# Down product of a split-precision feed-forward layer: right operands split where they are made, sums evicted by three engines

## The chip, the cores and the metric

The kernel runs on one core of a Trainium2 chip. The metric is device time in microseconds (us); the kernel before took 2532.09 us (median of three runs, 2531.11 to 2537.94).

## The reference

One encoder layer over two groups of sequences (256 and 1024 tokens, each with 16 learned meta tokens ahead), width D = 1024, everything in float32. The change lies in the two feed-forward halves:

```python
h = h + 0.5 * _swiglu(_rmsnorm(h, norm_ffn1), ffn1_w_gate, ffn1_w_up, ffn1_w_down)
...                                   # u = rmsnorm(h) @ w_in; attention and pooling; h += mix @ w_out
h = h + 0.5 * _swiglu(_rmsnorm(h, norm_ffn2), ffn2_w_gate, ffn2_w_up, ffn2_w_down)
h = _rmsnorm(h, norm_final)

def _swiglu(x, w_gate, w_up, w_down):         # w_gate, w_up: 1024 x 2816, w_down: 2816 x 1024
    return (jax.nn.silu(x @ w_gate) * (x @ w_up)) @ w_down
```

## The kernel before

**Precision.** A float32 product is three matmuls (`mm3`, lines 161 to 163): each operand is a sum of a high part (a cast to the format fp32r) and a low part (the operand minus its high part), and high times high, low times high and high times low are accumulated. The high part of an operand is a cast on ScalarE (`hi_act`, line 146), the low part a subtraction on VectorE (`lo_dve`, line 152) or GpSimd (`lo_pool`, line 155). The pair of instructions is called a split below.

**Seven products.** Each of gate, up and down is done as a fast two by two block product with 7 products in place of 8 (`seven`, line 441): the operands' quarters are combined by sums and differences (weights in `s_parts`, right operands named b11, t1, t2, b22, t3, b21, t4 in that order), and the results are combined in place. `PRODUCTS` gives each product one of the accumulators A, B, C: A takes b11, t2, t3 and t4 in turn, C takes t1 and b22, so that a sum must be read out of PSUM before the next product may add to the same bank. Right operands come in two halves, s = 0 and 1, of two token groups each; one tile is 128 by 324 (first layer half, FFN1) or 128 by 320 (FFN2). Reading a sum out of its PSUM bank is called an eviction.

**Gate and up** (`gate_up`, line 457). 11 passes j, each of a gate and an up product (14 weight parts, 84 matmuls for each half and product). The first three j run for one half at a time (half 0 first, and half 1 after the other eight), beside which the right operands of the other half are formed; the other eight run for both. `after` in `product` drains sums by ScalarE (line 503) or adds them on VectorE (line 509); `up` multiplies by the gate and forms the down product's right operands b11 to t4, each of which goes to device memory as one float32 tile (`out`, line 469; the names hid_d4b and hid_d4t in rows are such tiles of j = 4: b for b11, b22 and b21, t for t1 to t4).

**Down** (`down_tasks`, line 532; the loop is `run_`). The 11 j make six slices: slice 0 holds one j (j = 3), slices 1 to 5 two each. In a slice, 4 blocks mp of two output chunks of 128 follow one another, each with 7 products and two halves: 84 matmuls, 42 in slice 0. A block splits its seven weight parts (ring buffers `wh`, `wl`, and the sums `ws`), and every product's sums go into h in SBUF by one VectorE instruction, h = 0.5 * bank + h (line 616, `after`); `ADDS` says which part of h: b11 and b21 share one, t1 and t3, t2 and b22. Each right operand is loaded as float32 (`load`, line 539, tile `raw`, four buffers, SP's queue) and split (`split`) into pool `x` (10 slots, for five operands of the second j in a slice) or `y` (32 slots in FFN1, 26 in FFN2). `work` does one load and split behind each product in the first three blocks of a slice, and four behind each in the last, and the rest after it. Since slots of `x` and most of `y` come free only as the slice's last block uses them, most splits of a slice lie at its border with the slice ahead.

**Order.** The kernel is written as one stream of instructions for a scheduler that gives each engine its own order from priorities and the times that buffers come free; what follows from that is shown in rows of the order below. All loads and writes named here are issued by SyncE (SP), in one queue, in order: an issue that waits holds those behind it.

## Time and profile before

| what | value |
|---|---|
| median of three runs | 2532.09 us |
| profiled execution, its own time | 2531.91 us |
| its span | 2529.8 us |
| granted clock of TensorE, mean | 0.963 |
| TensorE (PE) busy, matmuls | 2325.6 us (92%) |
| VectorE (DVE) busy | 1753.6 us (69%) |
| ScalarE (ACT) busy | 985.5 us (39%) |
| GpSimd (POOL) busy | 274.8 us (11%) |
| data moved | 308.48 MB, mean 122 GB/s |

The span is the time from the first to the last instruction of the profiled execution; 2.1 us of its own time lie around it. FFN1's gate and up passes run from the start to about 627 us, its down product from there to about 940; the mixer with attention follows, then FFN2's gate and up passes, and its down product from 2177 us to the end. A stretch is read as: its length, then each engine's busy time with the count of its instructions, the clock granted to TensorE as a share of the full one, the share of the DMA engines' time and the rate. An engine's busy time over a stretch's length says how much room it has there.

### The profile page before, as it was taken

The numbers are of one execution on the slowest core, as the hardware profiler recorded it, in microseconds if no ns is written. First come the engines' busy times: TensorE is split into PE (matmuls) and PEld (weight loads), VectorE is DVE, ScalarE is ACT, GpSimd is POOL, SyncE is SP. The second block draws the span as 40 slices with busy tenths as digits, with TensorE's granted clock in tenths as the row PEclk, the third lists the DMA queues.
The fourth block names the chain that finished last, engine by engine and source line by source line (L and its number), as shares of the span: only waits on it lengthen the run. The fifth ranks groups of instructions, "written<-read, shape, count | busy, mean of one in ns | idle before, by whom it ended". The sixth has DMA issues, their size and how long they took to land.

```text
span 2529.8 us, 42335 instructions
## 1 busy us (share of the span) xinstructions
PE 2325.6 (92%) x15434; PEld 2264.9 (90%) x15434; DVE 1753.6 (69%) x3850; ACT 985.5 (39%) x2247; POOL 274.8 (11%) x342
## 2 busy tenths in 40 slices
PE   5899999999799998999888898899999999888897
PEld 5899999999699998899878898889999999788897
DVE  6965546558999996443477747685465557898997
ACT  6533333334433343111366733353333334433433
POOL 0000000000000013111366743000000000000000
PEclk7999999999899998999999999999999999999998
DMA  8323222354544423563654154432223227434432
GB/s 226 117 88 111 79 81 95 108 175 143 145 128 112 116 92 95 154 215 101 176 138 127 48 160 153 132 109 87 84 98 100 71 87 237 135 117 126 127 102 84
DMA packets 351236, 308.48 MB, mean 122 GB/s; under 512 B 29004, under 2 KB 337316, under 8 KB 350516
## 3 DMA queue, kind: packets, MB, share of 16 engines
q1 hardware_dynamic: 351028, 305.79, 39.9%
q8 instruction: 121, 1.98, 0.3%
q14 instruction: 87, 0.71, 0.1%
HBM read 212.55 MB, written 97.37 MB: 123 GB/s over the span
## 4 chain that ended last, share of the span: by engine, by line
PE 69%; DVE 14%; DMA 9%; ACT 3%; issue 3%; POOL 2%; SPq 1%; ACTq 0%; POOLq 0%; DVEq 0%
PE bank L162 22%; PE bank L161 22%; PE bank L163 21%; DVE h L616 3%; DVE wl L152 3%; DMA v<-v_d 2%; ACT wh L146 1%; DVE yl L152 1%; PE pair L957 1%; DMA wraw<-in_ffn_w_up 1%; PE bank L1005 1%; PE pair L958 1%; PE bank L242 1%; DVE xl L152 1%; DMA wraw<-in_ffn_w_gate 1%
## 5 line engine op out<-in xcount | busy, mean ns | idle before, releaser
L152 DVE TENSOR_TENSOR wl<-wraw,wh 128x512 fp32r<-128x512 f32 (+2 forms) x374 | 220.8, 600 | 271.7 <-ACT wh L146 216.6
L146 ACT CAST wh<-ws 128x512 fp32r<-128x512 f32 (+2 forms) x414 | 211.7, 513 | 448.9 <-PE bank L163 256.5
L162 PE MATMUL bank<-yh,wl 128*128 128x324 f32 (+1 forms) x1128 | 358.1, 318 | 16.5 <-DVE wl L152 16.4
L161 PE MATMUL bank<-yh,wh 128*128 128x324 f32 (+1 forms) x1128 | 341.6, 321 | 25.8 <-DVE h L616 12.0
L163 PE MATMUL bank<-yl,wh 128*128 128x324 f32 (+1 forms) x1128 | 353.4, 315 | 0.0
L616 DVE SCALAR_TENSOR_TENSOR h<-bank,h 128x324 f32<-128x324 f32 (+1 forms) x672 | 321.4, 489 | 30.8 <-PE bank L163 24.2
L152 DVE TENSOR_TENSOR wl<-ws,wh 128x512 fp32r<-128x512 f32 (+2 forms) x414 | 229.5, 557 | 79.0 <-ACT wh L146 77.2
L161 PEld LDWEIGHTS bank<-yh,wh 128*128 128x128 f32 x1128 | 211.5, 193 | 40.5 <-ACT wh L146 15.0
L162 PEld LDWEIGHTS bank<-yh,wl 128*128 128x128 f32 x1128 | 217.0, 192 | 23.8 <-DVE wl L152 21.8
L503 ACT COPY hid<-bank 128x324 f32<-128x324 f32 (+1 forms) x264 | 112.8, 428 | 291.2 <-PE bank L163 260.9
L163 PEld LDWEIGHTS bank<-yl,wh 128*128 128x128 f32 x1128 | 216.4, 192 | 0.6 <-POOL yl L155 0.5
L509 DVE TENSOR_TENSOR hid<-bank,hid 128x324 f32<-128x324 f32 (+1 forms) x264 | 129.4, 490 | 83.7 <-PE bank L163 77.2
L146 ACT CAST wh<-wraw 128x512 fp32r<-128x512 f32 (+2 forms) x310 | 153.6, 513 | 47.5 <-PE bank L163 40.1
L162 PE MATMUL bank<-xh,wl 128*128 128x324 f32 (+1 forms) x472 | 152.1, 323 | 17.6 <-DVE wl L152 17.6
L161 PE MATMUL bank<-xh,wh 128*128 128x324 f32 (+1 forms) x472 | 148.2, 324 | 5.5 <-DVE h L616 3.8
L163 PE MATMUL bank<-xl,wh 128*128 128x324 f32 (+1 forms) x472 | 150.2, 319 | 0.0
L161 PE MATMUL bank<-t1h,wh 128*128 128x324 f32 (+1 forms) x352 | 112.3, 320 | 19.9 <-ACT wh L146 19.9
L146 ACT CAST yh<-raw 128x324 fp32r<-128x324 f32 (+1 forms) x188 | 84.8, 460 | 104.2 <-DMA raw<-hid_d4b 11.6
L223 POOL TENSOR_TENSOR ry<-rv,neg_half 81x4 f32<-81x4 f32 (+3 forms) x12 | 13.5, 1124 | 979.8 <-DVE rv L235 979.8
L162 PE MATMUL bank<-t1h,wl 128*128 128x324 f32 (+1 forms) x352 | 113.1, 321 | 3.4 <-DVE wl L152 3.2
L161 PE MATMUL bank<-t2h,wh 128*128 128x324 f32 (+1 forms) x352 | 110.6, 314 | 4.6 <-ACT hid L503 3.0
L161 PE MATMUL bank<-t4h,wh 128*128 128x324 f32 (+1 forms) x352 | 109.4, 311 | 5.3 <-DVE hid L509 5.3
(258 smaller groups left out, 6782.4 us busy)
## 6 DMA issues: line engine op xcount, KB each, us to landing
wraw<-in_ffn_w_gate SPq DMA_DIRECT2D x56, 512.0 KB
wraw<-in_ffn_w_up SPq DMA_DIRECT2D x56, 512.0 KB
wraw<-in_ffn_w_down SPq DMA_DIRECT2D x88, 256.0 KB
k<-k_d SPq DMA_DIRECT2D x32, 260.0 KB
wraw<-in_w_in SPq DMA_DIRECT2D x16, 512.0 KB
wraw<-in_w_out SPq DMA_DIRECT2D x16, 512.0 KB
h<-h_d SPq DMA_DIRECT2D x8, 648.0 KB
h_d<-h SPq DMA_DIRECT2D x10, 512.0 KB
```

The lines of the kernel that those rows point to most:

```text
L146: nc.scalar.copy(out=out, in_=in_)
L152: nc.vector.tensor_sub(out, in_, hi.bitcast(F32))
L161: nc.tensor.matmul(out=ps, lhsT=wh, rhs=xh, start=first, stop=False, skip_group_check=on)
L162: nc.tensor.matmul(out=ps, lhsT=wl, rhs=xh, start=False, stop=False, skip_group_check=on)
L163: nc.tensor.matmul(out=ps, lhsT=wh, rhs=xl, start=False, stop=last, skip_group_check=on)
L242: nc.tensor.matmul(out=ps[:, j * m : (j + 1) * m], lhsT=r[:, j : j + 1].broadcast_to([m, P]), rhs=ident[:m, :m], start=True, stop=True,)
L503: nc.scalar.copy(out=kept[s, name], in_=ps)
L509: nc.vector.tensor_add(t, ps, t)
L616: nc.vector.scalar_tensor_tensor(out=hs, in0=ps, scalar=0.5, in1=hs, op0=ALU.mult, op1=ALU.add)
L957: nc.tensor.matmul(out=ps[:, m], lhsT=qs, rhs=kh[:, ks], start=True, stop=False)
L958: nc.tensor.matmul(out=ps[:, m], lhsT=qs, rhs=kl[:, ks], start=False, stop=True)
L1005: nc.tensor.transpose(out=psv[:kn, j, :], in_=s_["l", 0][:, k0 : k0 + kn], identity=ident)
```

## The change

**Splits.** `out` in `gate_up` casts each operand on ScalarE into a new tile `hu` (3 or 4 buffers), writes it, subtracts it in place on GpSimd, and writes the rest: the high and the low part stand side by side in device memory (`[P, 2, m]`). The writes of b11, b22, t1 now come together, after t2 is formed, and those of t2, b21, t4 together at the end. Buffers `hid` go from 9, 18 and 10 to 8, 16 and 9. The down product loads both parts with one DMA (332 KB) straight into a slot, with no split behind it; `work`, `plan`, `fetch` and `raw` are gone. Slots: `x` 10 as before, and two pools `a` and `b` of 18, used by slices in turn.

**Sums.** The sums of b11, t1 and t2 (both halves) leave PSUM by ScalarE, times 0.5, into a tile `nt` (4 buffers), and GpSimd adds this to h. Those of b22, t3, b21 and t4 go by VectorE as before (line 597 now).

**Weights.** Two weight parts (four in slice 0) share one tile of the ring; the two extra pairs `eh`, `el` of slice 0 are gone.

**Round about.** The mixer's operands `xm` take their slots from `a` and `b`; FFN2 closes `b` before the last slice and loads the final norm's gain there (it was loaded ahead of the down product); `vh` in the mixer has two buffers in place of three.

```diff
-    def s_parts(a11, a12, a21, a22, tp, extra=None):
+    def s_parts(a11, a12, a21, a22, tp):
...
+        box = {}
         def tiles():
-            if extra and count[0] < 2:
-                wh, wl = (extra.tile([P, 2, P], F32R, tag=t, name=t, bufs=2) for t in ("eh", "el"))
-            else:
-                wh, wl = (ring.tile([P, 4, P], F32R, tag=t, name=t, bufs=RING) for t in ("wh", "wl"))
+            i = count[0] % (4 // k) * k
             count[0] += 1
-            return wh[:, :k], wl[:, :k]
+            if i == 0:
+                box["w"] = [ring.tile([P, 4, P], F32R, tag=t, name=t, bufs=RING) for t in ("wh", "wl")]
+            return tuple(w[:, i : i + k] for w in box["w"])
...
         def out(s, key, t):
-            nc.sync.dma_start(out=hid[j][key][s], in_=t)
+
+            u = tp.tile([P, NS], F32R, tag="hu", name="hu", bufs=hu)[:, :n].bitcast(F32)
+            hi_act(u.bitcast(F32R), t)
+            nc.sync.dma_start(out=hid[j][key][s][:, 0], in_=u)
+            nc.gpsimd.tensor_sub(t, t, u)
+            nc.sync.dma_start(out=hid[j][key][s][:, 1], in_=t)
...
-            if key != "b12":
-                out(s, key, b)
...
-                out(s, "t1", t1)
                 t2 = x[s, "t2"] = temp()
                 nc.vector.tensor_sub(t2, x[s, "b22"], t1)
-                out(s, "t2", t2)
+                for k, t in (("b11", b), ("b22", x[s, "b22"]), ("t1", t1)):
+                    out(s, k, t)
             elif key == "b21":
-                t4 = temp()
-                nc.vector.tensor_sub(t4, b, x[s, "t2"])
-                out(s, "t4", t4)
+                t4, t2 = temp(), x[s, "t2"]
+                nc.vector.tensor_sub(t4, b, t2)
+                for k, t in (("t2", t2), ("b21", b), ("t4", t4)):
+                    out(s, k, t)
...
+    SLOTS = dict(x=2 * len(IN_X), a=18, b=18)
+
+    BY_POOL = ("b11", "t1", "t2")
...
-        def load(i, name, s, jj):
-            raw = st.tile([P, NS], F32, tag="raw", name="raw", bufs=4)[:, :n]
-            nc.sync.dma_start(out=raw, in_=hid[slices[i][jj]][name][s])
-            return raw
-
-        def split(i, name, s, jj, where, raw):
-            th, tl = T[i][s, name][jj] = slot(where)
-            hi_act(th, raw)
-            lo_dve(tl, raw, th)
+        def load(i, name, s, jj, where):
+            t = pools_[where].tile([P, 2, NS], F32R, tag=f"h{where}", name=f"h{where}", bufs=SLOTS[where])[:, :, :n]
+            nc.sync.dma_start(out=t.bitcast(F32), in_=hid[slices[i][jj]][name][s])
+            T[i][s, name][jj] = t[:, 0], t[:, 1]
...
-            return [(i, *k, "y") for k in ys], [(i, *k, "x") for k in xs]
+            return deque((i, *k, "ba"[i % 2]) for k in ys), deque((i, *k, "x") for k in xs)
...
-            ys, xs = lists(0)
-            plan(xs + ys)
-            work(len(xs))
+            box["ys"], xs = lists(0)
+            for k in xs:
+                load(*k)
             box["raw"] = raw_w(0, 0)
 
-        def run_(done):
-            work(len(T_NAMES) * 2 - 2 * len(IN_X))
...
+        def run_(done, close_b):
+            for k in box["ys"]:
+                load(*k)
...
-                        nc.vector.scalar_tensor_tensor(out=hs, in0=ps, scalar=0.5, in1=hs, op0=ALU.mult, op1=ALU.add)
+                        if name in BY_POOL:
+                            t = temp()[:, :n]
+                            nc.scalar.mul(out=t, in_=ps, mul=0.5)
+                            nc.gpsimd.tensor_add(hs, hs, t)
+                        else:
+                            nc.vector.scalar_tensor_tensor(out=hs, in0=ps, scalar=0.5, in1=hs, op0=ALU.mult, op1=ALU.add)
...
                             if mp < KC // 2 - 1:
-                                work(1)
+                                if ys:
+                                    load(*ys.popleft())
                             else:
-                                work(4)
-                                plan(q.popleft() for q in (ys, xs, ys, xs) if q)
-                                fetch()
+                                for _ in range(2):
+                                    if xs:
+                                        load(*xs.popleft())
```

SyncE, around the start of FFN1's down product. Before (hid_d3b and hid_d3t are the operands of slice 0, loaded to be split; w_up and w_gate are weights of gate and up passes, w_down those of the down product):

```order
L469 DMA hid_d0t_96<-hid 128x324
L539 DMA raw<-hid_d3b_132 128x324
L539 DMA raw<-hid_d3t_133 128x324
L168 DMA wraw<-in_ffn_w_up 128x8x128
L539 DMA raw<-hid_d3t_134 128x324
L539 DMA raw<-hid_d3b_135 128x324
L577 DMA wraw<-in_ffn_w_down 128x2x256
L539 DMA raw<-hid_d3b_136 128x324
L539 DMA raw<-hid_d3t_137 128x324
L539 DMA raw<-hid_d3t_138 128x324
L168 DMA wraw<-in_ffn_w_gate 128x8x128 x2
```

After (hid_d2b and hid_d2t are written by the last gate and up pass, hu being the high part; hid_d3b_135 to hid_d3t_138 are b21 and t4 of slice 0, both halves; ha and hb are slots of the pools):

```order
L472 DMA hid_d2t_116<-hu 128x324
L474 DMA hid_d2t_116<-hid 128x324
L472 DMA hid_d2b_122<-hu 128x324
L474 DMA hid_d2b_122<-hid 128x324
L472 DMA hid_d2t_124<-hu 128x324
L474 DMA hid_d2t_124<-hid 128x324
L543 DMA ha<-hid_d4b_140 128x648
L543 DMA ha<-hid_d4t_141 128x648
L543 DMA hb<-hid_d3b_135 128x648
L543 DMA hb<-hid_d3b_136 128x648
L543 DMA hb<-hid_d3t_137 128x648
L543 DMA hb<-hid_d3t_138 128x648
```

The four loads of b21 and t4 stood before the last pass's first weights; now they stand behind all of that pass's writes.

VectorE, in a block in the middle of FFN1's down product. Before (yl is the low part of a right operand, wl that of a weight part, ws a weight sum):

```order
L616 SCALAR_TENSOR_TENSOR h<-bank,h 128x324
L152 TENSOR_TENSOR wl<-ws,wh 128x256
L616 SCALAR_TENSOR_TENSOR h<-bank,h 128x324
L152 TENSOR_TENSOR yl<-raw,yh 128x324
L616 SCALAR_TENSOR_TENSOR h<-bank,h 128x324
L426 TENSOR_TENSOR ws<-wraw,ws 128x256
L616 SCALAR_TENSOR_TENSOR h<-bank,h 128x324
L152 TENSOR_TENSOR wl<-ws,wh 128x256
L616 SCALAR_TENSOR_TENSOR h<-bank,h 128x324
L152 TENSOR_TENSOR yl<-raw,yh 128x324
L152 TENSOR_TENSOR wl<-ws,wh 128x256
L616 SCALAR_TENSOR_TENSOR h<-bank,h 128x324
```

After, the rows that hold one block's evictions:

```order
L597 SCALAR_TENSOR_TENSOR h<-bank,h 128x324 x2
L152 TENSOR_TENSOR wl<-ws,wh 128x256
L152 TENSOR_TENSOR wl<-wraw,wh 128x256
L597 SCALAR_TENSOR_TENSOR h<-bank,h 128x324
L420 TENSOR_TENSOR ws<-ws,wraw 128x256
L597 SCALAR_TENSOR_TENSOR h<-bank,h 128x324 x3
L152 TENSOR_TENSOR wl<-wraw,wh 128x256
L597 SCALAR_TENSOR_TENSOR h<-bank,h 128x324 x2
L152 TENSOR_TENSOR wl<-wraw,wh 128x256
L152 TENSOR_TENSOR wl<-ws,wh 128x256
L426 TENSOR_TENSOR ws<-wraw,ws 128x256
```

The splits are gone from VectorE's row, and 8 evictions are left of 14.

GpSimd, from the last gate and up pass into slice 0, after (line 473 is the subtraction of a high part, line 595 the add of a drained sum to h; before, GpSimd has no instruction here):

```order
L473 TENSOR_TENSOR hid_7237<-hid_7237,hu_7349 128x324
L595 TENSOR_TENSOR h_6398<-h_6398,nt_7428 128x324
L473 TENSOR_TENSOR hid_7260<-hid_7260,hu_7354 128x324
L595 TENSOR_TENSOR h_6398<-h_6398,nt_7431 128x324
L473 TENSOR_TENSOR hid_7280<-hid_7280,hu_7359 128x324
L595 TENSOR_TENSOR h_6398<-h_6398,nt_7450 128x324
L595 TENSOR_TENSOR h_6398<-h_6398,nt_7453 128x324
L595 TENSOR_TENSOR h_6398<-h_6398,nt_7468 128x324
L473 TENSOR_TENSOR hid_7347<-hid_7347,hu_7383 128x324
L595 TENSOR_TENSOR h_6398<-h_6398,nt_7471 128x324
L473 TENSOR_TENSOR hid_7214<-hid_7214,hu_7388 128x324
L473 TENSOR_TENSOR hid_7381<-hid_7381,hu_7393 128x324
```

The six adds of slice 0's first block stand between the subtractions of the last pass; one more subtraction stands right ahead of these rows.

## Rows read from the trace of the kernel before

**Rows 1.** Page, parts 1 and 4: busy us (share) xinstructions; the chain by engine.

```profile
PE 2325.6 (92%) x15434; PEld 2264.9 (90%) x15434; DVE 1753.6 (69%) x3850; ACT 985.5 (39%) x2247; POOL 274.8 (11%) x342
...
PE 69%; DVE 14%; DMA 9%; ACT 3%; issue 3%; POOL 2%; SPq 1%; ACTq 0%; POOLq 0%; DVEq 0%
```

**Rows 2.** Stretches, three blocks: us, PE, PEld, DVE, ACT, POOL, clock, DMA share, GB/s.

```profile
2266.20:2280.80 14.60, 13.88 (x95) 13.62 (x94) 14.12 (x36) 9.12 (x22) 0.00 (x0) 1.00 0.56 160
2280.80:2298.60 17.80, 13.85 (x78) 12.73 (x77) 14.40 (x38) 6.41 (x17) 0.00 (x0) 0.90 0.59 173
2298.60:2310.80 12.20, 12.20 (x85) 12.20 (x84) 11.91 (x33) 3.78 (x11) 0.00 (x0) 1.00 0.21 66
```

**Rows 3.** Stretches: slice 0, slices 1 to 4, start of slice 5; both products.

```profile
627.40:676.70 49.30, 35.14 (x180) 31.24 (x178) 45.65 (x128) 20.95 (x60) 0.00 (x0) 0.86 0.51 150
676.70:896.10 219.40, 207.97 (x1338) 200.47 (x1338) 205.28 (x514) 87.39 (x222) 0.00 (x0) 0.99 0.44 123
896.10:934.40 38.30, 38.02 (x255) 37.49 (x254) 37.36 (x92) 16.61 (x44) 4.97 (x6) 1.00 0.15 45
2177.00:2225.50 48.50, 33.98 (x170) 28.20 (x169) 43.47 (x125) 17.45 (x52) 0.00 (x0) 0.89 0.49 149
2225.50:2450.30 224.80, 208.18 (x1353) 202.72 (x1353) 206.33 (x513) 88.23 (x223) 0.00 (x0) 0.98 0.40 119
2450.30:2478.20 27.90, 25.91 (x162) 25.04 (x161) 24.80 (x63) 7.97 (x21) 0.00 (x0) 0.94 0.15 49
```

**Rows 4.** Groups by shape, 640 to 940 us; L503 (page); L155 (ns min/median/max).

```profile
L616 DVE SCALAR_TENSOR_TENSOR h<-bank,h 128x324 f32<-128x324 f32 x312 | 151.0, 491 | 10.6 <-PE bank L163 7.2
...
L152 DVE TENSOR_TENSOR yl<-raw,yh 128x324 fp32r<-128x324 f32 x85 | 41.4, 488 | 0.5 <-ACT yh L146 0.4
...
L146 ACT CAST yh<-raw 128x324 fp32r<-128x324 f32 x84 | 38.4, 462 | 59.3 <-DMA raw<-hid_d6t 6.8 <-DMA raw<-hid_d10b 6.2 <-DMA raw<-hid_d1t 5.8
...
L503 ACT COPY hid<-bank 128x324 f32<-128x324 f32 (+1 forms) x264 | 112.8, 428 | 291.2 <-PE bank L163 260.9
...
L155 POOL TENSOR_TENSOR yl<-nt,yh x16: 876/887/1317, 953.9 to 1008.4; 128x324 fp32r<-128x324 f32 x16
```

**Rows 5.** Timeline at 919 us: start, us, engine, line; VectorE, then GpSimd.

```profile
919.32 1.01 DVE L434 TENSOR_TENSOR ws<-wraw 128x256 f32<-128x256 f32 x1
...
920.25 1.11 DVE L152 TENSOR_TENSOR wl<-ws,wh 128x256 fp32r<-128x256 f32 x1
...
921.28 0.48 DVE L616 SCALAR_TENSOR_TENSOR h<-bank,h 128x324 f32<-128x324 f32 x1
...
921.69 0.41 DVE L417 TENSOR_TENSOR ws<-wraw 128x256 f32<-128x256 f32 x1
...
919.16 1.91 POOL L260 TENSOR_TENSOR acc<-acc,nt 128x324 f32<-128x324 f32 x2 [867.01 <-ACT nt L259]
```

**Rows 6.** Stretches of gate and up passes: four of one half, one of both.

```profile
78.00:112.10 34.10, 29.32 (x170) 27.57 (x170) 31.92 (x67) 18.03 (x38) 0.00 (x0) 0.90 0.46 134
112.10:141.40 29.30, 27.03 (x170) 25.17 (x169) 25.75 (x50) 13.30 (x28) 0.00 (x0) 1.00 0.40 126
1636.20:1672.50 36.30, 29.65 (x172) 26.80 (x173) 34.75 (x73) 18.57 (x41) 0.00 (x0) 0.95 0.39 119
2151.90:2177.00 25.10, 24.79 (x169) 24.44 (x168) 19.99 (x43) 12.96 (x30) 0.00 (x0) 1.00 0.35 113
292.50:342.50 50.00, 50.00 (x338) 50.00 (x337) 27.32 (x52) 16.59 (x34) 0.00 (x0) 1.00 0.28 90
```

**Rows 7.** Chain, start and us; SP queue timeline; the stretch with most DMA.

```profile
2178.01 2.42 DMA raw<-hid_d4b
...
2181.47 4.89 DMA raw<-hid_d4t
...
558.01 0.97 SPq L539 DMA_DIRECT2D raw<-hid_d3b  x2
...
540.00:560.00 20.00, 16.89 (x100) 16.14 (x99) 13.69 (x25) 6.70 (x14) 0.00 (x0) 0.91 0.96 336
```

More of the change, by code (lines that the diff above doesn't have):

```diff
@@ L260, in norm_sq, with norm_tasks @@
         (nc.vector if m % 2 else nc.gpsimd).tensor_add(acc[b], acc[b], sq)
-    def norm_tasks(key, hb, n, cols, gain, slot, temp, out, gaps):
+    def norm_tasks(key, hb, n, cols, gain, slots, temp, out, gaps):
         m = n // 4
@@ L273, in part @@
         def part(c):
-            xh, xl = slot("y")
+            xh, xl = next(slots)
             out.append((xh, xl))
@@ L551, in lists @@
             xs = [(name, s, two) for name in IN_X for s in range(2)]
-            return [(i, *k, "y") for k in ys], [(i, *k, "x") for k in xs]
-        ahead = deque()
-        def plan(keys):
-            todo.extend(keys)
-        def fetch():
-            while todo and len(ahead) < 4:
-                key = todo.popleft()
-                ahead.append((key, load(*key[:4])))
-        def work(k=1):
-            for _ in range(k):
-                fetch()
-                if not ahead:
-                    return
-                key, raw = ahead.popleft()
-                split(*key, raw)
-            fetch()
+            return deque((i, *k, "ba"[i % 2]) for k in ys), deque((i, *k, "x") for k in xs)
         def raw_w(i, mp):
@@ L639, in run_ @@
                         seven(s_parts(*quads, st), rhs, n, (0, 1), after)
-                        if mp == KC // 2 - 1:
-                            assert not ys and not xs
-                            work(len(todo) + len(ahead))
+                assert not ys and not xs
         return head_x, run_, slot
@@ L769, in encoder @@
     pools_ = {"x": xpool}
-    first, down, slot = down_tasks(h, places, NS, hid1_d, a["ffn1_w_down"][0], pools_, 32, hp, SINGLE1)
+    first, down, slot = down_tasks(
+        h, places, NS, hid1_d, a["ffn1_w_down"][0], pools_, hp, lambda: temp1("nt"), SINGLE1
+    )
     def load_h(h, src, n):
@@ L782, in encoder @@
             first()
[L783 removed]
+        gate_up(j, T, NS, (1,), wg, wu, hid1_d, tp, 9, 3)
     pump(len(tasks))
@@ L786, in encoder @@
     t1st.close()
-    xst, pools_["y"] = scope("hidy")
+    xst, pools_["a"], pools_["b"] = scope("hida", "hidb")
+    xm_slots = (slot("b" if k < 18 else "a") for k in range(4 * KC))
     xm = [[] for _ in BS1]
     acc = {}
-    def temp1(tag):
-        return tp1.tile([P, NS], F32, tag=tag, name=tag, bufs=2 if tag == "nt" else 1)
     def h_part(c, b):
@@ L808, in to_mix @@
             tasks.append((("h", s), lambda: nc.sync.dma_start(out=h_d[:, :, lo - META : hi - META], in_=h[:, :, lo:hi])))
-    down(to_mix)
+    down(to_mix, lambda: None)
     dst.close()
@@ L1405, in encoder @@
         pools_ = {"x": xpool}
-        first, down, _ = down_tasks(h, places, n, hid2_d, a["ffn2_w_down"][0], pools_, 26, hp, SINGLE2)
+        first, down, _ = down_tasks(
+            h, places, n, hid2_d, a["ffn2_w_down"][0], pools_, hp,
+            lambda: hp.tile([P, NS], F32, tag="nt", name="nt", bufs=4), SINGLE2
+        )
         tasks.extend(spread(("h", 0), load_h(h, h2_d, T2 // 2), 8))
```

71 lines of the change are left out of this document (35 added, 36 removed).

## The prediction, made before the changed kernel ran

> **What bounds the kernel now.** I read the page's engine line first, then the chain. TensorE is busy 92% of the span and holds 69% of the chain; VectorE holds 14% [rows 1]. So the question is where TensorE waits, and I looked for that stage by stage, in stretches. In a gate and up pass of both halves (292.5 to 342.5 us) it issues 338 matmuls in 50.0 us, 148 ns each, with VectorE at 27.3 us of 50 [rows 6]: nothing to gain there. The down products are different. One block (7 products, two halves, 84 matmuls) in the middle of a slice takes 12.2 us with TensorE full and VectorE at 11.9; the blocks on either side of a slice's border take 14.6 and 17.8, with VectorE at 14.1 and 14.4 and TensorE at 13.9 [rows 2]. VectorE works at the pace of TensorE, so the ten splits that gather at a border stop TensorE.
>
> Summed [rows 3]: slices 1 to 4 take 219.4 us in the first product; 16 blocks at 12.3 (324 columns) are 196.8, so 22.6 are lost. Three blocks of slice 5 lose 38.3 - 36.9 = 1.4. In the second product 224.8 - 16 x 12.2 = 29.6, and two blocks lose 27.9 - 24.4 = 3.5. **Together 57 us.** Slice 0 holds half the work, 168 matmuls x 148 ns = 24.9 us, and takes 49.3 and 48.5: 48 us more are lost. I count it by itself, since the change acts otherwise there.
>
> **The change, part by part.**
>
> *Splits leave the down products.* Per block of two, VectorE now does 14 evictions, 11 weight operations and 7 to 8 splits: 33 instructions in 11.91 us, 0.36 each [rows 2]. It will have 8 evictions and 11 weight operations, 19 x 0.36 = 6.9 us of 12.3. ScalarE: 7 casts of weights at no more than 0.46 (the larger yh cast's time) and 6 drains at 0.43 [rows 4], 5.8 us. GpSimd: 6 adds at 0.887, 5.3 us (at most 6 x 1.317 = 7.9) [rows 4]. None reaches 12.3 alone.
>
> *GpSimd beside VectorE.* With an add on GpSimd, weight operations of VectorE took 1.01 and 1.11 us, against 0.41 of the same shape alone; the eviction between them, from PSUM, 0.48 as ever; two GpSimd adds took 1.91, 0.95 each [rows 5]. So an add takes 0.6 to 0.7 from VectorE where a weight operation is due, six times a block at most: 6.9 + 6 x 0.65 = 10.8 us. Still under 12.3, but no longer by much. The Trainium skill (SBUF — State Buffer, § Who interferes with whom) says that a VectorE instruction with two SBUF inputs and a GpSimd instruction that reads SBUF exclude each other, the later one blocking fully. By that an add could take its whole 0.887: 6.9 + 5.3 = 12.2, no slack, and I would give 0.5 us a block back, some 20 us in all (an estimate); the rows show the milder 0.65, since the start of an instruction overlaps the one before.
>
> *The order of the sums.* b22 goes onto a part of h that t2 goes onto just before, so b22's eviction on VectorE waits for GpSimd's add, and t3's and b21's stand behind it; t4's matmuls need t3's eviction. Half a product is 0.88 us here. The first sum is ready at 0.88, drained at 1.4; six adds end at 1.4 + 6 x 0.95 = 7.1. Then b22's second eviction, two weight splits and t3's eviction, 0.4 to 0.5 each, end at 9.0; t4 starts at 10.6. It fits, with 1.6 us to spare. I leave 8 us over the 39 blocks, for the first block of each slice and for collisions: **57 becomes 8, a gain of 49** (bounds 25 to 57).
>
> *Loads.* A slice fetches 28 tiles of 332 KB in place of 166 KB and 2 MB of weights, 11.3 MB in 49 us, 230 GB/s; the chip has moved 336 over 20 us [rows 7]. Each tile has a slot of the other pool, or (t3 and the four before, of the second in a pair) is fetched some 10 us ahead of use. I take nothing (bounds 0, and 3.4 us a slice if only 215 of the 336 were to be had).
>
> *Slice 0.* Here a gain is uncertain, and I followed the order by hand, from the end of the last gate and up pass (t = 0). In SP's queue the four tiles that products b21 and t4 of the first block need now stand behind the last pass's writes, and the last of these waits for GpSimd's subtraction of t4. On GpSimd 13 operations stand from b11's subtraction to that one, among them all six adds of the first block. The first can start at about 0 and runs 0.9 each: t = 11 to 12. Four more issues at 0.49 [rows 7] and 2.4 us to land (4.9 the worst [rows 7]) give t = 15 to 16 for tiles wanted at t = 4.4. Then 1.8 us for b21 and t4, to 18; and three blocks that are bound by a chain, since half a product is only 0.44 here: 0.44, drain 0.43, six adds 5.3, evictions of b22 (one) and t3 (two) 1.5, t4's 0.9: 8.5 us, 25.5 in all. End: t = 43.5, against 49.3 and 48.5. **Gain 5 each, 10 together** (bounds: 38 together, where tiles are there in time and blocks take 7; a loss of 10, where the last write waits 10 us more).
>
> *Writes in the gate and up passes.* Each of 308 tiles gets a cast on ScalarE (0.46), a subtraction on GpSimd (0.89) and a second write. In passes of both halves this is 14 a pass: ScalarE from 16.6 to 23 of 50 us, GpSimd 12.4, VectorE 27.3 + 14 x 0.65 = 36.4 [rows 6]. All of it lies beside TensorE's 50. Queued behind the casts on ScalarE are the drains of the next product; with 3.5 us to a product they have time. Passes of one half take 25 us where nothing waits, and those beside which the second half's operands are formed take 34.1, 29.3 and 36.3 with VectorE at 31.9, 25.8 and 34.8: it is the bound there [rows 6]. Three times 7 subtractions fall into these stretches, and each takes 0.5 (the mean of 0.6, 0.7 and collisions that cost nothing): **+10 us** (bounds 0 and 21 x 0.89 = 19). At the later one-half passes VectorE has 5 us free (20.0 of 25.1), and loses 4: +2 (bounds 0 and 8).
>
> *The rest* (other slots for the mixer's operands, one vh buffer fewer, final gain loaded later, weights two products to a slot) I cost at nothing: the matmuls of w_in and the transposes cover it; without this cover the tail's 52 us could move by 4 either way. Weights ready a block ahead are a help that the 49 already holds.
>
> **Sum.** 2531.9 (the profiled execution: its span 2529.8 and 2.1 around it, beside a median of 2532.1) - 49 - 10 + 10 + 2 = **2485 us**.
>
> **Rivals.**
> 1. *Slice 0 is cured.* The order says that the four tiles wait for GpSimd; but if the subtractions come earlier than I worked out, slice 0 falls to 30 us. For it: VectorE's evictions and splits, 45.7 of 49.3 us there [rows 3], are mostly gone. Against: the order of SP's queue. 2485 - 28 = 2457.
> 2. *The chain over GpSimd sets the block.* Slower. In every block t4's matmuls wait for t3's eviction, this one behind b22's, that one for the sixth add. If adds take p, t3 is evicted at 1.4 + 6p + 1.9, plus 1.3 if the two splits between collide too. It decides from p = 1.2 (0.99 with the collisions). GpSimd took 1.317 once, 0.887 in the middle [rows 4], 0.95 in a pair [rows 5]. At p = 1.25 with collisions the block is 12.3 + 1.5 = 13.8: 39 x 1.5 = 59 in place of my 8, giving 2536; with b22's wait pushing the weights as well, 14.0 and 2543.
> 3. *ScalarE is held by writes.* With 3 or 4 buffers for the high part, a cast waits until a write four back has landed, and drains and weights stand behind it. For it: 2.4 to 4.9 us to land [rows 7]; against: drains have 3.5 us. At 1.2 us for each of 28 passes, +34: 2519.
> 4. *The change halves no wait, because loads take the place of splits:* 3.4 us in each of 10 slices, +34: 2519. Against: 230 of 336 GB/s.
>
> **How the numbers follow.** About 0.3% (7.6 us) can be told from no change here. Chances: forecast 0.56; slice 0 cured 0.13; chain over GpSimd 0.14 (0.10 beyond 2540, 0.04 within); ScalarE held 0.11 (0.07 faster, 0.04 within); loads 0.06 (faster). Faster: 0.56 + 0.13 + 0.07 + 0.06 = 0.82; same 0.04 + 0.04 = 0.08; slower 0.10. The forecast's own range is 2465 to 2506. To 8 in 10 it has to reach the middle of the cured case and both cases at 2519, up to where the chain over GpSimd begins: 2453 to 2526.
>
> **What would show it.** Right: blocks in the middle and at the borders of slices alike at 12.2 to 12.5 us; VectorE at 7 to 11 us a block; in slice 0 a stop of some 10 us before b21's matmuls, released by the load of hb, then blocks of 8 us; passes at 78 and 1636 us longer by 3 to 5. Wrong: borders that still take 15 us (then the splits were not the cause), matmuls that wait for line 597 in every block (rival 2), for drains in the gate and up passes (rival 3) or for hx and ha (rival 4).

## The result: slower by 0.7%

The changed kernel takes 2551.34 us (median of 4 runs, 2550.36 to 2552.34); before 2531.95 (4 runs). The ratio is 1.0071, 95% interval 1.0054 to 1.0089. The forecast was 2485, range 2453 to 2526: wrong in sign. The profiled execution took 2550.51 us, its span 2548.7, against 2531.91 and 2529.8: 18.9 us of span to explain.

The engine line of the page after, which answers to [rows 1]:

```profile
PE 2318.8 (91%) x15434; PEld 2272.9 (89%) x15434; DVE 1703.2 (67%) x3254; ACT 1084.2 (43%) x2535; POOL 868.5 (34%) x938
```

VectorE lost 596 instructions and only 50 us of busy time; GpSimd gained 596 instructions and 594 us. To see where the time went, I measured each stage in both traces: a pass from the end of the last VectorE add of a sum (line 509 before, 513 after) in one pass to that in the next, a block from the end of the last VectorE eviction (line 616, 597) of one block to that of the next:

| stage, both products (us) | before | after | difference | forecast |
|---|---|---|---|---|
| passes of one half, and the pass behind the first three (12 stretches) | 396.3 | 455.4 | **+59.1** | +12 |
| the other passes of both halves (14 stretches) | 694.7 | 700.6 | +5.9 | 0 |
| slice 0 | 102.0 | 98.8 | -3.2 | -10 |
| slices 1 to 4 | 444.2 | 401.1 | **-43.1** | -49, with slice 5 |
| slice 5 and the tail | 136.2 | 139.9 | +3.7 | (above) |
| first pass, mixer | 756.3 | 752.9 | -3.4 | 0 |

The first row holds passes 2 to 4 and 12 to 14 of each product (the first pass stands with the mixer; pass 4 runs both halves, but starts behind a pass of one half). So the down product gave 42.6 us of the 59 that were forecast, and the gate and up passes took it all back, and more.

Stretches after, columns as in [rows 2]. First, four passes of one half (before 28.8, 25.9, 25.0 and 24.3 us by the same measure), then one of both halves ([rows 6] has its like), slice 0's last three blocks, and two blocks on either side of a border between slices ([rows 2]):

```profile
112.90:147.10 34.20, 28.51 (x166) 26.59 (x165) 29.76 (x48) 16.56 (x36) 8.61 (x8) 0.90 0.44 141
1691.50:1722.70 31.20, 28.00 (x169) 27.28 (x169) 23.92 (x36) 14.78 (x32) 7.83 (x8) 0.89 0.50 159
2163.10:2192.50 29.40, 27.06 (x171) 26.35 (x170) 20.26 (x36) 13.04 (x29) 7.72 (x7) 0.94 0.66 213
2192.50:2223.00 30.50, 25.45 (x166) 24.21 (x165) 26.43 (x50) 16.77 (x43) 8.15 (x7) 1.00 0.42 136
353.70:404.60 50.90, 50.17 (x338) 49.90 (x337) 31.29 (x52) 21.63 (x49) 14.70 (x15) 1.00 0.42 134
679.60:705.00 25.40, 19.84 (x125) 18.73 (x124) 14.84 (x34) 9.14 (x24) 15.41 (x18) 0.97 0.75 269
2360.40:2372.70 12.30, 12.30 (x86) 12.30 (x85) 9.18 (x21) 4.99 (x14) 5.52 (x6) 1.00 1.01 330
2372.70:2385.00 12.30, 12.30 (x86) 12.30 (x85) 9.16 (x20) 4.92 (x14) 5.50 (x6) 1.00 1.06 364
```

This border is cured: 12.3 us with TensorE full, where [rows 2] has 14.6 and 17.8, and DMA at 364 GB/s keeps up. (Only the first block behind slice 0 stays long, at 16.0 and 13.6 us in the two products.) Each pass of one half is some 5 us longer, though VectorE is idle for 4 to 9 us in it. The pass of both halves, with 15 operations of GpSimd, takes 1.0 more than its like before (49.9).

What happens in such a pass stands at its border. VectorE and GpSimd, groups by shape in the pass from 2192.5 us (columns as in [rows 4]):

```profile
L473 POOL TENSOR_TENSOR hid<-hid,hu 128x320 f32<-128x320 f32 x7 | 8.1, 1184 | 20.7 <-ACT hu L146 18.8 <-DVE hid L485 1.5 <-ACT hid L507 0.5
L152 DVE TENSOR_TENSOR wl<-ws,wh 128x512 fp32r<-128x512 f32 x8 | 6.7, 853 | 0.2
L513 DVE TENSOR_TENSOR hid<-bank,hid 128x320 f32<-128x320 f32 x7 | 3.4, 485 | 1.4 <-PE bank L163 1.2 <-issue 0.2
L426 DVE TENSOR_TENSOR ws<-wraw,ws 128x512 f32<-128x512 f32 x2 | 2.1, 1032 | 0.0
```

The same groups of the kernel before, in its last pass from 2151.0 us:

```profile
L152 DVE TENSOR_TENSOR wl<-ws,wh 128x512 fp32r<-128x512 f32 x8 | 5.5, 686 | 0.9 <-ACT wh L146 0.7
L509 DVE TENSOR_TENSOR hid<-bank,hid 128x320 f32<-128x320 f32 x7 | 3.4, 489 | 1.8 <-PE bank L163 1.7
L426 DVE TENSOR_TENSOR ws<-wraw,ws 128x512 f32<-128x512 f32 x2 | 1.4, 686 | 0.0
```

Weight operations grew from 0.686 to 0.85 and 1.03 on the mean; the operation with one operand in PSUM kept its 0.485. The Trainium skill (SBUF — State Buffer, § Who interferes with whom) says that of VectorE's instructions those with two SBUF inputs contend with a GpSimd instruction that reads SBUF, and those with at most one, outside VectorE's 2-port modes, don't; these rows agree as to which are lengthened. Here is the timeline of VectorE, and GpSimd, at that border (start, us), with the waits of TensorE in the pass:

```profile
2193.04 1.17 DVE L478 TENSOR_TENSOR hid<-hid 128x320 f32<-128x320 f32 x1
...
2194.13 0.68 DVE L420 TENSOR_TENSOR ws<-ws,wraw 128x512 f32<-128x512 f32 x1
...
2195.53 1.02 DVE L487 TENSOR_TENSOR hid<-hid 128x320 f32<-128x320 f32 x1
...
2196.47 0.68 DVE L152 TENSOR_TENSOR wl<-ws,wh 128x512 fp32r<-128x512 f32 x1
...
2196.68 3.56 POOL L473 TENSOR_TENSOR hid<-hid,hu 128x320 f32<-128x320 f32 x3 [0.48 <-ACT hid L507]
2197.08 1.15 DVE L492 TENSOR_TENSOR hid<-hid 128x320 f32<-128x320 f32 x1
...
2198.15 1.37 DVE L426 TENSOR_TENSOR ws<-wraw,ws 128x512 f32<-128x512 f32 x1
```

```profile
PE bank L162 <- DVE wl L152: 5.0, 3, 2.9
```

In the first 9 us VectorE must do the sums of the pass that ended (lines 478 to 492) and the next pass's first weight parts (417 to 434, 152). All seven subtractions of the pass that ended start there too, 0.2 to 9.0 us behind the border, and TensorE waits for the weights' low parts: 5.0 us in three waits. This pass grew by 6.2 us, from 24.3 to 30.5. Not all of that need be collision: VectorE's order changed here as well, and the low part that TensorE waits for longest stands behind four operations on the ended pass's operands since its last add, where it stood right behind that add before. At the border at 112.9 us the order is the one before, operations are lengthened all the same (a weight's low part to 1.36 us), and the pass is 5.4 us longer than before.

### The profile page after: what moved, and what is told of

It reads as the page before. It is cut to its first block, busy times and chain, and to the rows that moved or that the text cites. A ratio compares the mean times of both kernels' runs of the same rounds, so it can differ in the third digit from the quotient of the medians.

```text
span 2548.7 us, 43346 instructions
## 1 busy us (share of the span) xinstructions
PE 2318.8 (91%) x15434; PEld 2272.9 (89%) x15434; DVE 1703.2 (67%) x3254; ACT 1084.2 (43%) x2535; POOL 868.5 (34%) x938
## 5 line engine op out<-in xcount | busy, mean ns | idle before, releaser
L473 POOL TENSOR_TENSOR hid<-hid,hu 128x324 f32<-128x324 f32 (+1 forms) x308 | 328.1, 1089 | 896.5 <-ACT hu L146 846.8
L595 POOL TENSOR_TENSOR h<-h,nt 128x324 f32<-128x324 f32 (+1 forms) x288 | 266.0, 942 | 305.1 <-ACT nt L594 302.5
L146 ACT CAST hu<-hid 128x324 fp32r<-128x324 f32 (+1 forms) x308 | 138.1, 461 | 192.7 <-DVE hid L481 68.0
L597 DVE SCALAR_TENSOR_TENSOR h<-bank,h 128x324 f32<-128x324 f32 (+1 forms) x384 | 174.7, 483 | 62.3 <-PE bank L163 36.2
L161 PE MATMUL bank<-hb,wh 128*128 128x324 f32 (+1 forms) x536 | 171.0, 320 | 36.8 <-DMA hb<-hid_d3b 25.2
L161 PE MATMUL bank<-ha,wh 128*128 128x324 f32 (+1 forms) x600 | 189.4, 317 | 7.2 <-DVE h L597 3.3
L162 PE MATMUL bank<-ha,wl 128*128 128x324 f32 (+1 forms) x600 | 189.3, 316 | 1.7 <-DVE wl L152 1.7
L163 PE MATMUL bank<-ha,wh 128*128 128x324 f32 (+1 forms) x600 | 188.1, 314 | 0.0
L162 PE MATMUL bank<-hb,wl 128*128 128x324 f32 (+1 forms) x536 | 169.3, 316 | 0.9 <-DVE wl L152 0.9
L163 PE MATMUL bank<-hb,wh 128*128 128x324 f32 (+1 forms) x536 | 168.4, 316 | 0.3 <-POOL hb L155 0.2
L161 PE MATMUL bank<-hx,wh 128*128 128x324 f32 (+1 forms) x480 | 152.0, 317 | 3.0 <-ACT nt L594 2.9
L162 PE MATMUL bank<-hx,wl 128*128 128x324 f32 (+1 forms) x480 | 150.4, 313 | 0.0
L163 PE MATMUL bank<-hx,wh 128*128 128x324 f32 (+1 forms) x480 | 150.2, 313 | 0.0
```

The costliest lines, as they stand in the source:

```text
L146: nc.scalar.copy(out=out, in_=in_)
L161: nc.tensor.matmul(out=ps, lhsT=wh, rhs=xh, start=first, stop=False, skip_group_check=on)
L162: nc.tensor.matmul(out=ps, lhsT=wl, rhs=xh, start=False, stop=False, skip_group_check=on)
L163: nc.tensor.matmul(out=ps, lhsT=wh, rhs=xl, start=False, stop=last, skip_group_check=on)
L473: nc.gpsimd.tensor_sub(t, t, u)
L595: nc.gpsimd.tensor_add(hs, hs, t)
```

## Experiments

The runs after the first comparison were made on three chips, on each of which the kernel before took 2522 to 2523 us; so times are compared as ratios to the kernel before, run on the same chip, and by the lengths of stages, each from one profiled execution. Stage sums of all runs stand in one table behind the single runs.

**e1: writes only; e2: no subtraction.**

```diff
         def out(s, key, t):
...
-            hi_act(u.bitcast(F32R), t)                           # e1 only
-            nc.sync.dma_start(out=hid[j][key][s][:, 0], in_=u)   # e1: in_=t
-            nc.gpsimd.tensor_sub(t, t, u)                        # e1, e2
             nc.sync.dma_start(out=hid[j][key][s][:, 1], in_=t)
```

> The changed kernel without the cast on ScalarE and the subtraction on GpSimd in the gate and up passes: each operand is written twice as it is, so the low part is wrong and the output is not the reference's; writes, loads, queue order and the down product are as in the changed kernel. The changed kernel's twelve one-half passes and the borders to the full ones take 58 us longer than before. Theory A (GpSimd's subtractions beside VectorE lengthen VectorE's work at the passes' borders) and theory B (ScalarE is held by the casts, whose hu buffers wait for writes) both expect these 58 us to go: about 2551 - 55 = 2496. Theory C (the doubled writes and their place in SP's queue) expects them to stay: 2540 to 2551.

> The changed kernel with cast and both writes, but without GpSimd's subtraction in the passes (the low part that is written is the whole operand, so the output is not the reference's). Theory A (collision of GpSimd with VectorE) expects about the time of the kernel that only writes, 2495 to 2505. Theory B (ScalarE held by casts that wait for a hu buffer) expects most of the loss to stay: 2530 to 2551. Between them, the share of the 58 us that goes is A's.

e1: 0.9834 of before (0.9806 to 0.9863). e2: 0.9854 (0.9787 to 0.9922; its two runs lie 14 us apart). The third and the last pass of one half in e2:

```profile
110.50:139.20 28.70, 26.24 (x166) 24.58 (x166) 25.32 (x49) 16.10 (x36) 0.00 (x0) 1.00 0.54 170
2140.90:2165.50 24.60, 23.33 (x154) 22.35 (x153) 20.50 (x47) 15.62 (x40) 0.00 (x0) 1.00 0.50 164
```

28.7 and 24.6, as before the change, with all casts on ScalarE (16.1 us busy) and all writes still there. Of the 59.1 us, e2 gives back 455.4 - 411.9 = 43.5: that is GpSimd's subtractions. The six passes of one half in each product have 84 of them, **0.52 us each**; counted by where they start, 98 fall into the twelve stretches, 0.44 each. They don't cost the same everywhere: the two stretches behind the passes of both halves lose 0.4 together (40.1 and 39.3 us after, 40.4 and 38.6 in e2), the other ten 1.2 to 5.9 each. The remaining 15.6 is all the rest of the change in these passes (casts, doubled and later writes, fewer buffers), 10.4 of it in those two stretches (e9, below). Casts alone are no cause of any size: e1, without them, is 4 us shorter in these passes.

The twelve stretches together, the changed kernel and then e2:

```profile
sum 455.40, PE 384.55 PEld 371.02 DVE 343.46 ACT 213.93 POOL 104.96; mean PE 32.05 PEld 30.92 DVE 28.62 ACT 17.83 POOL 8.75
```

```profile
sum 411.80, PE 368.20 PEld 355.69 DVE 301.27 ACT 211.18 POOL 0.00; mean PE 30.68 PEld 29.64 DVE 25.11 ACT 17.60 POOL 0.00
```

With the subtractions VectorE is busy for 42.2 us more, with nearly the same number of instructions (594 and 590). TensorE stands idle for 27.2 us more (length less busy time), and its matmuls, nearly the same number (2381 and 2376), take 16.4 us more. The mean granted clock of these stretches, which mixes the clock's two levels, is 0.92, in e2 0.97. So over a third of the loss is matmuls that run slower.

**e3: the subtraction on VectorE; e8: on GpSimd, half the columns.**

```diff
-            nc.gpsimd.tensor_sub(t, t, u)
+            nc.vector.tensor_sub(t, t, u)                                             # e3
+            nc.gpsimd.tensor_sub(t[:, : n // 2], t[:, : n // 2], u[:, : n // 2])      # e8
```

> The changed kernel with the subtraction in the passes on VectorE in place of GpSimd: 7 times 0.49 = 3.4 us more of VectorE's own work in a one-half pass, and no GpSimd beside it. Theory A: a GpSimd subtraction costs VectorE 0.6 to 0.7 where they collide, so this one is cheaper or equal, 2520 to 2545, with passes of one half at 27 to 29 us where nothing but VectorE's own work stands at the border. Theory B: no gain, 2548 to 2560, since ScalarE's casts stay and VectorE has more to do.

> The changed kernel, where GpSimd's subtraction in the passes covers only the first half of the columns (the other half's low part is left wrong, so the output is not the reference's): the count of instructions, writes and waits is the changed kernel's, the time of each subtraction about half. If the time that GpSimd is busy beside VectorE is the cost: some half of the 58 us of the one-half passes goes, 25 to 35 us below the change. The rival, that one more step between operand and write at the border is the cost, however short: within 8 us of the change in these passes.

e3: 0.9994 (0.998 to 1.0008); e8: 0.9985 (0.9971 to 1.0). The last passes in e3 and e8:

```profile
2166.50:2196.10 29.60, 26.62 (x161) 26.00 (x161) 24.61 (x56) 16.51 (x42) 0.00 (x0) 0.88 0.42 140
```

```profile
2168.90:2196.70 27.80, 25.35 (x162) 24.78 (x161) 24.13 (x50) 16.94 (x43) 5.55 (x8) 0.94 0.45 149
```

The twelve stretches together, e3 and then e8:

```profile
sum 439.00, PE 381.17 PEld 369.45 DVE 342.94 ACT 215.51 POOL 0.00; mean PE 31.76 PEld 30.79 DVE 28.58 ACT 17.96 POOL 0.00
```

```profile
sum 440.50, PE 384.78 PEld 371.62 DVE 317.19 ACT 213.57 POOL 71.78; mean PE 32.06 PEld 30.97 DVE 26.43 ACT 17.80 POOL 5.98
```

With half the columns a subtraction takes 5.55 / 8 = 0.69 in place of 8.15 / 7 = 1.16 us in the last pass. The loss above e2 falls from 43.5 to 440.5 - 411.9 = 28.6, so 14.9 us come back: less than the 25 to 35 that I expected, more than the rival's 8. What TensorE stands idle above e2 falls from 27.2 to 12.1, much as VectorE's added time does (42.2 to 15.9); what its matmuls lose does not fall (16.4 and 16.6). So the time of a subtraction counts; that the number of steps counts for nothing is not shown. On VectorE itself, with no GpSimd beside it, the loss is 438.9 - 411.9 = 27.0, 0.32 a tile. VectorE's added time there is 41.7, as in the change: the border has no free time on VectorE for this work in either form. Why GpSimd's form loses 16.5 more is open; VectorE's order differs between the two as well. e3's expectation was met in its total, though this pass took 29.6 and not 27 to 29.

One border of e8 shows another way to lose, the pass at 112.8 us. Its row, all subtractions of e8 (ns min/median/max), and a wait in this pass:

```profile
112.80:146.00 33.20, 28.04 (x166) 25.89 (x166) 25.39 (x49) 16.46 (x36) 9.50 (x8) 0.95 0.45 144
...
L473 POOL TENSOR_TENSOR hid<-hid,hu x308: 516/661/5715, 76.7 to 2207.3; 128x162 f32<-128x162 f32 x77, 128x160 f32<-128x160 f32 x77
...
ACT hu L146 <- POOL hid L473: 3.6, 1, 3.6
```

Here VectorE kept its pace (0.50 and 0.70 us an operation), and GpSimd gave way: one subtraction took 5.7 us, beside 11 operations of VectorE on two SBUF operands. ScalarE's next cast waited 3.6 us for it to free a buffer `hu`, the weights' casts stood behind that one, and TensorE waited 2.6 us for them. The pass is 4.5 us longer than in e2, with hardly any of it on VectorE.

**e4: all sums by VectorE, splits as changed; e5: sums as changed, splits left in the down product.** Two parts of the change, each alone.

```diff
-    BY_POOL = ("b11", "t1", "t2")
+    BY_POOL = ()                            # e4, from the changed kernel
```

```diff
+                        if name in ("b11", "t1", "t2"):       # e5, from the kernel before
+                            t = temp()[:, :n]
+                            nc.scalar.mul(out=t, in_=ps, mul=0.5)
+                            nc.gpsimd.tensor_add(hs, hs, t)
+                        else:
                             nc.vector.scalar_tensor_tensor(out=hs, in0=ps, scalar=0.5, in1=hs, op0=ALU.mult, op1=ALU.add)
```

> The changed kernel with all seven sums evicted by VectorE; only the splits stay out of the down product. My account of the down product has the splits as the cause of its lost time: 14 evictions and 11 weight operations are 25 x 0.36 to 0.42 = 9 to 10.5 us of 12.3 in a block, so blocks of two stay at 12.3 to 12.5; slice 0's blocks are then bound by VectorE, 14 x 0.48 + 11 x 0.25 = 9.5 us in place of 8.3, and its first block loses its chain over GpSimd. Total 2545 to 2562. The rival, that the eviction by three engines carries the gain, expects blocks of 13 us and more: 40 x 0.7 = 28 us slower or worse, 2575 and up.

> The kernel before with one part of the change alone: sums of b11, t1 and t2 leave PSUM by ScalarE and GpSimd, and all splits stay in the down product (nt 4 buffers; FFN2's y pool 24 slots in place of 26). By the last runs the eviction by three engines costs some 24 us against eviction by VectorE when the splits are gone. Theory A (an add on GpSimd takes about as much from VectorE by collision as the eviction that it saves, and its chain holds slice 0's blocks): no gain, 0.998 to 1.015 of before (2527 to 2570 on the scale of 2532). The rival (VectorE is what holds the borders, so that any relief of six evictions, 2.9 us a block, gives time back there): 0.985 to 0.992.

e4: 0.9977 (0.9965 to 0.999), 24 us below the changed kernel's 1.0071. That is 2526 on the scale where before is 2532, less than the 2545 to 2562 that I expected. e5: 1.0132 (1.0098 to 1.0167), slower than before by 34 us. The eviction by three engines costs by itself, with the splits or without them. (In e5 `nt` has four buffers, and FFN2's pool `y` 24 slots in place of 26. The slots are not the cause: slices 1 to 4 of FFN1's product, with its 32 as before, lost 14 us, those of FFN2's 6.) e4, slice 0's last three blocks, and the block behind a border; then two blocks of e5, one behind a border, one in a slice's middle:

```profile
674.80:695.50 20.70, 19.75 (x129) 18.88 (x128) 20.42 (x54) 1.61 (x7) 0.00 (x0) 1.00 0.89 322
...
2283.30:2295.50 12.20, 12.20 (x86) 12.20 (x85) 10.15 (x25) 2.48 (x8) 0.00 (x0) 1.00 1.06 365
```

```profile
2302.00:2318.30 16.30, 11.90 (x72) 10.36 (x71) 16.12 (x33) 9.49 (x26) 6.42 (x6) 1.00 0.56 160
2332.10:2343.60 11.50, 11.50 (x81) 11.50 (x80) 9.06 (x21) 4.83 (x14) 5.88 (x6) 1.00 0.14 47
```

With 14 evictions on VectorE and no splits, the border block is 12.2 us with VectorE at 10.15: six evictions more than in the changed kernel, and 1 us more of busy time (9.16 there). In e5 VectorE is full at the border again (16.12 of 16.30). Why six evictions less give so little shows in the groups of the first down product. The changed kernel from 700 to 900 us, then e4 in the same stretch:

```profile
L152 DVE TENSOR_TENSOR wl<-ws,wh 128x256 fp32r<-128x256 f32 x66 | 44.6, 691 | 37.9 <-ACT wh L146 37.8
...
L434 DVE TENSOR_TENSOR ws<-wraw 128x256 f32<-128x256 f32 x16 | 15.6, 975 | 0.0
```

```profile
L152 DVE TENSOR_TENSOR wl<-ws,wh 128x256 fp32r<-128x256 f32 x69 | 27.7, 421 | 0.0
...
L434 DVE TENSOR_TENSOR ws<-wraw 128x256 f32<-128x256 f32 x16 | 6.6, 415 | 0.0
```

Six evictions at 0.49 were taken from VectorE, 2.9 us a block, and 1.9 of it came back as slower weight operations, while a chain over GpSimd was added. In e5, where VectorE is full at the borders, 19.9 of the 34.3 us that the down products lose fall into slices 1 to 4. In the changed kernel, whose blocks of two run at TensorE's pace, only 3.6 of its 27.6 us above e4 do; 16.5 are slice 0, where the chain of six adds sets a block, and 7.5 slice 5 with the tail. My own expectation for e4 had slice 0's blocks at 9.5 us, since I took 0.25 us a weight operation on top of 14 x 0.48. They took 6.1 to 8.3, 20.7 for three.

**e6, e7: raw halves.** The operands of the three passes j of one half (j = 0 to 2) are written once, as float32, as before, and split in the down product; the other eight stay split in the passes. The slices are arranged so that each has one raw j at most, whose 14 tiles are loaded and split one by one behind the sums of the slice ahead. The diff leaves out that the raw operands are written as soon as each is formed, as before, that the passes of one half have 9 and 10 buffers `hid` again, and that e7 has `BY_POOL = ()`.

```diff
+        plain = len(subs) == 1
         def out(s, key, t):
+            if plain:
+                nc.sync.dma_start(out=hid[j][key][s][:, 1], in_=t)
+                return
...
+        slices = [[3], [4, 5], [0, 6], [1, 7], [2, 8], [9, 10]]
...
+        def split(keep):
+            if len(pend) > keep:
+                t = pend.popleft()
+                hi_act(t[:, 0], t[:, 1].bitcast(F32))
+                lo_dve(t[:, 1], t[:, 1].bitcast(F32), t[:, 0])
```

> The changed kernel, where the operands of the three j that run one half at a time are written once, as float32, as before, and split in the down product; the eight passes of both halves split as in the change. Slices are [3], [4,5], [0,6], [1,7], [2,8], [9,10], so that each slice has at most one raw j, whose 14 splits are spread over the slice ahead. If the split's place in the one-half passes is the loss: these passes come back to their length of before, 58 us less than the change; the 14 splits for each of three slices find room beside 19 other instructions of VectorE a block and cost 0 to 10. About 2496 on the scale where before is 2532, 0.984 to 0.990 of before. The rival, that the down product has no room for them beside GpSimd's adds: 0.992 to 1.0.

> The same, with all sums evicted by VectorE as before. If the three-engine eviction costs 24 to 28 us by itself in slice 0, in the first blocks and at the end of the down products: 24 to 28 us below the one with three engines, about 2470, 0.973 to 0.979 of before. The rival: 14 evictions, 11 weight operations and 5 splits, 30 x 0.41 = 12.3 us, fill VectorE in the slices that carry raw operands, which then lose 1 to 2 us a block as the borders did before: 9 blocks in each product, 10 to 30 us, 2480 to 2500, no better than with three engines.

e6: 0.9944 (0.9927 to 0.9961), outside what I expected of it and inside the rival's 0.992 to 1.0. e7, with evictions by VectorE: **0.9755** (0.9732 to 0.9777), as expected. In both the passes of one half are back at 410 to 412 us, as in e2. In e6 the down products take 648.7, in e7 605.2: with GpSimd's adds beside it, VectorE has no room for the splits (the blocks that carry them take 14.6 to 17.1 us in the second product's slice 1), and without them it has. e7 at the place of e5's block behind a border, and in a slice's middle:

```profile
2237.30:2250.20 12.90, 12.90 (x90) 12.90 (x89) 11.87 (x33) 6.94 (x17) 0.00 (x0) 1.00 0.93 304
2261.80:2274.10 12.30, 12.30 (x86) 12.30 (x85) 11.77 (x31) 2.77 (x9) 0.00 (x0) 1.00 0.14 47
```

The rival for e7 (VectorE full, 1 to 2 us a block lost) falls: 31 instructions take 11.77 us of 12.3, TensorE is full, and slices 1 to 4 take 398.6 us, 1.1 more than in e4, which has no splits there.

**e9, e10: the last pass of both halves raw as well; then one sum, t1, by three engines.** In e7 one pass was still long, the first of one half behind the passes of both (40 us against 34). VectorE's first weight sum there waits for buffers that are being written out (waits of e7, 540 to 560 us):

```profile
PE bank L161 <- ACT wh L146: 10.0, 1, 10.0
DVE ws L417 <- DMA hid_d10t<-hid: 6.7, 1, 6.7
```

```diff
-        plain = len(subs) == 1
+        plain = len(subs) == 1 or j == NF // 2 - 1
-        slices = [[3], [4, 5], [0, 6], [1, 7], [2, 8], [9, 10]]
+        slices = [[3], [4, 5], [0, 6], [1, 7], [2, 8], [10, 9]]
...
+    BY_POOL = ("t1",)                       # e10 only
```

> The version with raw halves and evictions by VectorE, and the last pass of both halves (j = 10) written raw as well, its splits in the down product's fourth slice. At the border behind that pass TensorE stands 10 us, as VectorE's first weight sum waits for buffers that are still being written to device memory (28 writes of pass 10 where 14 were before); this pass border is 6 us longer than before in both products. Expected if the doubled writes are the cause: 4 to 6 us less twice, 8 to 12 us below the version with raw halves, 2450 or 0.971 of before. The rival, that the loads of h in the same queue hold these writes anyway: no difference (within 3 us).

> The same with one sum of seven, t1, evicted by ScalarE and GpSimd. If any add on GpSimd costs VectorE more than it saves: 3 to 15 us slower than with none. The rival, that only the chain of six adds is too long and a single product's share relieves VectorE in the blocks that carry raw splits (13 to 14 us in place of 12.3): 2 to 6 us faster.

e9: **0.9726** (0.9709 to 0.9742), the fastest: 2451.3 us where before takes 2522.6. That pass falls from 40.4 to 35.9 and from 39.9 to 34.3, 10.1 us together, so what was done to pass 10's operands is the cause. Which part of it is less clear, since e9 takes away casts, subtractions and late writes along with the doubled ones. The subtractions cost nothing here (above). In e1, with doubled writes and neither casts nor subtractions, the two stretches take 38.6 and 35.5 us, where before has 33.9 and 34.7 and e2, with the casts, 40.4 and 38.6: by these single profiles the writes are about half of it and the casts the rest. e10: 0.9734 (0.9715 to 0.9754); the two can't be told apart by their times, and neither theory of e10 is settled. By stages, slice 0 is 4.8 us shorter in e10 and slices 1 to 4 are 6.5 longer.

All runs by stage (us of the profiled execution, both products; "down" from the end of the last pass, with the tail; "rest" is the first pass and the mixer):

| kernel | one-half passes | other passes | down | rest | ratio to before |
|---|---|---|---|---|---|
| before | 396.3 | 694.7 | 682.4 | 756.3 | 1 |
| after | 455.4 | 700.6 | 639.8 | 752.9 | 1.0071 |
| e1 writes only | 408.0 | 693.9 | 625.1 | 750.3 | 0.9834 |
| e2 no subtraction | 411.9 | 694.8 | 631.0 | 751.9 | 0.9854 |
| e3 subtraction on VectorE | 438.9 | 692.3 | 639.3 | 751.6 | 0.9994 |
| e8 half a subtraction | 440.5 | 694.5 | 636.9 | 749.8 | 0.9985 |
| e4 sums by VectorE | 454.1 | 697.6 | 612.2 | 742.9 | 0.9977 |
| e5 sums by three, splits left | 395.2 | 694.8 | 716.7 | 747.1 | 1.0132 |
| e6 raw halves | 409.9 | 697.7 | 648.7 | 751.6 | 0.9944 |
| e7 raw halves, VectorE | 411.7 | 700.6 | 605.2 | 744.0 | 0.9755 |
| e9 and last pass raw | 401.6 | 696.8 | 603.7 | 743.7 | 0.9726 |
| e10 and t1 by three | 399.4 | 698.7 | 607.7 | 748.2 | 0.9734 |

The stages of down and of the passes are the argument here. The rest scatters from 743 to 756 us; no run was made to settle why, and nothing is concluded from it. e4's profiled execution was the shortest of its eight, and e2's the longer of its two, so their ratios are the better measure of their sums.

## Why the prediction was wrong

**Writes in the gate and up passes** is the step that failed: +12 forecast, 59.1 + 5.9 = +65 measured, 43.5 of it by the subtractions in the twelve stretches. I charged 0.5 us in full to 21 of 84 subtractions, in the stretches where VectorE was busy for nearly the whole length: 10 forecast, 14.7 measured there (the changed kernel less e2). I let the other 63 pass for 2 us because VectorE "has 5 us free" in its passes: 28.8 measured. That is slack of a whole pass. The subtractions don't spread over it: they come in one burst behind the pass's last sums, where VectorE prepares the weights that TensorE needs next, and there is no slack in those 9 us. That the mean over all 84 (0.52) lies so near my price of 0.5 is in part luck: my 0.5 was VectorE's time alone, and 16.4 of the 43.5 are matmuls at a lower granted clock, a term that the forecast does not have. The casts and writes, which I put at nothing there, cost 15.6 more, 10.4 of it where the next pass takes over buffers that are still being written. In passes of both halves the cover nearly held (+5.9 over 14 passes).

**The splits leave the down products** held in its mechanism: the forecast was 57 of lost time down to 8, a gain of 49 with slice 5; slices 1 to 4 gained 43.1, slice 5 and the tail lost 3.7, and borders between slices of two run at TensorE's pace. But the gain was credited to the change as a whole. By e4 and e5 it is two terms of opposite sign: without the eviction by three engines the down products gain 682.4 - 612.2 = 70.2 us, and that eviction loses 639.8 - 612.2 = 27.6 of that (716.7 - 682.4 = 34.3 where the splits stay). Nor was VectorE's time the question: I forecast 10.8 us a block with the adds, it is 9.16 with them and 10.15 without, and both leave room in 12.3. The second edit was never asked for its own worth.

**Slice 0** came as described, if not as large: -3.2 of -10 forecast. The chain of the second product's slice 0 (start, us):

```profile
2233.15 0.86 POOL hid L473
2234.03 0.32 SPq L474
2234.44 0.38 SPq L472
...
2236.40 0.52 SPq L543
2236.98 0.60 SPq L543
2237.63 6.14 DMA hb<-hid_d3b
2243.82 0.63 PE bank L161
...
2247.98 0.44 ACT nt L594
2248.49 5.25 POOL h L595 x6
2253.76 0.90 DVE h L597 x2
2254.71 0.42 PE bank L161
...
2256.91 5.10 POOL h L595 x6
```

The last subtraction, SP's queue of writes, then the load of b21: TensorE stands 13.7 us here and 11.5 in the first product, where I had said some 10. In e2, without subtractions, it stands 9.0 and 8.3, and slice 0 takes 89.4 us in place of 98.8. Then blocks of 8.3 to 8.8 us that are set by six adds (8.5 forecast). The load took 6.1 us, over the 4.9 that I had as the worst. In e7, where the last pass writes at once, slice 0's first block takes 12.9 and 16.1 us in place of 23.1 and 25.0.

**Rivals.** Rival 2 (the chain over GpSimd sets every block) is refuted for full blocks: 12.3 us, an add at 0.94; it holds in slice 0, and what makes three blocks of slice 5 longer than in e4 was not tested. Rival 3 (ScalarE held by writes, +34) is refuted in its size by e1 and e2: with casts and writes and no subtraction 15.6 us are left, and 3.9 of them go with the casts. A ScalarE that is held by GpSimd's subtraction, as in e8, was not among the rivals. Rival 4 (loads) is refuted by the border blocks at 330 to 364 GB/s. The slower side came by a way that was in none of the rivals, though its price stood in the text.

## What to carry to other kernels

Work that is moved off one stage's critical engine must be priced at the minute where it lands, not against the mean slack of the stretch: look at what the engine that gets it, and any engine whose operations it lengthens (here GpSimd lengthened VectorE's), have to do between the last operand of one pass and the first weight of the next. Where a change has two parts that relieve the same engine, work out each alone; here the second part undid over a third of what the first gave in the down products. And elementwise work on GpSimd was no free help here, beside a VectorE that works on two SBUF operands: it took 2.9 us a block off VectorE, and 1.9 came back.
